# Row-wise largest absolute value of an 8192 x 8192 matrix: SyncE's loads without the waits that VectorE's count implies

## Chip, cores and metric

One core of one Trainium2 chip. The metric is the device time of one execution in microseconds (us), the median over several; the trace's span leaves out some 1.8 us of it.

## The reference

```python
x = np.random.randn(8192, 8192).astype(np.float32)
out = np.linalg.norm(x, ord=np.inf, axis=1)     # per row: the largest |x|
```

## The kernel before

The matrix is read once, 256 MiB, in 8 MB tiles of 128 partitions x 16384 values (two rows for each partition). Three buffers hold them. SyncE issues every load, VectorE reduces each tile, two small stores write the result. The last eight tiles come in smaller and smaller pieces, so that little is left to reduce once the last byte is there.

```python
sbuf = ctx.enter_context(tc.tile_pool(name="sbuf", bufs=BUFS))      # BUFS = 3
...
for a in range(A):                                                  # 24 tiles in all: the bulk
    for n in range(G):
        t = sbuf.tile([P, W + PAD], F32, tag="t")
        nc.sync.dma_start(out=t[:, :W], in_=x_b[a, n])              # L147
        absmax(r_bulk[:, a, n * B : (n + 1) * B], t[:, :W].rearrange(...))
for i, loads in enumerate(TAIL):                                    # 7 tiles in pieces
    t = sbuf.tile([P, W + PAD], F32, tag="t")
    for j, w in enumerate(loads):
        nc.sync.dma_start(out=t[:, at : at + w], in_=x_t[i][:, at : at + w])   # L159
        ...                                                         # reduces into part
...                                                                 # last tile: 13 pieces, L184
nc.sync.dma_start(out=out_t, in_=r_tail[:])                         # L202, the last store
nc.at_finalize(start_first_load_early)
nc.at_finalize(finish_on_pool)
```

The waits are put in by the framework. A load into a used buffer has two kinds: for VectorE's count (the reduce of the old content is done) and for the semaphore of the load that brought that content. In this kernel's trace the loads count up eight DMA semaphores (100 to 107) in turn, and some loads also wait for the load that had their semaphore before. No load or store of SyncE carries more than one wait in that trace; the others sit in 30 EVENT_SEMAPHOREs, one ahead of each of 29 loads and of the last store.

## Time and profile before

| | before |
|---|---|
| time, median of 3 (lowest to highest) | 627.47 us (627.43 to 627.56) |
| span of the profiled run | 625.7 us |
| loads' queue, share of 16 DMA engines | 99.5% |
| VectorE busy | 88% |
| EVENT_SEMAPHOREs ahead of SyncE's loads and last store | 30 |

```profile
L140 DVE TENSOR_REDUCE r_bulk<-t 128x2 f32<-128x16384 f32 x24 | 413.3, 17220 | 69.7 <-DMA t<-in_x_dram 69.7
t<-in_x_dram SPq DMA_DIRECT2D x24, 40.7
q14 instruction: 2, 0.02, 0.0%
```

A reduce takes 17.22 us and VectorE then waits for data, 69.7 us in all. A load of 8 MB takes 40.7 us from issue to landing.

### The profile page before, as it was taken

How to read it: one execution, taken by the hardware profiler on the slowest of the kernel's cores; microseconds unless marked ns; L12 is line 12 of the kernel's file. 1: busy time of each engine (PE TensorE's matmuls, PEld its weight loads, DVE VectorE, ACT ScalarE, POOL GpSimd, SP SyncE). 2: the span in 40 equal slices, each digit the busy share in tenths (PEclk: the TensorE clock that was granted, in tenths of full speed). 3: DMA queues.
4: the chain of work that ended last, by engine and by line, in shares of the span. 5: the costliest groups of instructions: out<-in, count | busy, mean ns of one | idle time of the engine just before them, and what ended most of it. 6: DMA issues, size and time to landing. Idle time of an engine off the chain costs nothing.

```text
span 625.7 us, 205 instructions
## 1 busy us (share of the span) xinstructions
DVE 552.9 (88%) x67; POOL 0.2 (0%) x4
## 2 busy tenths in 40 slices
DVE  0588988889988889888898888988889999999998
POOL 0000000000000000000000000000000000000000
DMA  9999999999999999999999999999999999999997
GB/s 402 469 402 452 419 452 419 448 423 436 436 419 452 411 461 402 469 402 469 402 469 402 461 411 452 419 448 423 444 413 421 444 425 431 436 425 430 424 422 315
DMA packets 9282, 268.49 MB, mean 429 GB/s; under 512 B 1856, under 2 KB 1856, under 8 KB 3392
## 3 DMA queue, kind: packets, MB, share of 16 engines
q1 hardware_dynamic: 8496, 268.45, 99.5%
q10 hardware_dynamic: 784, 0.02, 0.1%
q14 instruction: 2, 0.02, 0.0%
HBM read 268.44 MB, written 0.03 MB: 429 GB/s over the span
## 4 chain that ended last, share of the span: by engine, by line
DMA 67%; DVE 31%; issue 1%; another core or an unknown queue 0%; DVEq 0%; SPq 0%
DMA t<-in_x_dram 67%; DVE r_bulk L140 24%; DVE part L140 6%; DVE t L140 2%; DVEq L230 0%; DVE r_tail L140 0%; SPq L159 0%
## 5 line engine op out<-in xcount | busy, mean ns | idle before, releaser
L140 DVE TENSOR_REDUCE r_bulk<-t 128x2 f32<-128x16384 f32 x24 | 413.3, 17220 | 69.7 <-DMA t<-in_x_dram 69.7
L140 DVE TENSOR_REDUCE part<-t 128x1 f32<-128x8192 f32 (+20 forms) x28 | 121.5, 4410 | 0.3 <-DMA t<-in_x_dram 0.3
L140 DVE TENSOR_REDUCE t<-t 128x1 f32<-128x1664 f32 (+8 forms) x11 | 16.7, 1576 | 0.2 <-DMA t<-in_x_dram 0.2
L140 DVE TENSOR_REDUCE r_tail<-t 128x1 f32<-128x644 f32 (+1 forms) x2 | 1.5, 814 | 0.0
L137 DVE MEMSET part<- 128x56 f32 x1 | 0.1, 105 | 0.9 <-PEq L219 0.9
L140 DVE TENSOR_REDUCE r_tail<-part 128x14 f32<-128x56 f32 x1 | 0.2, 201 | 0.0
L219 POOL MEMSET const-bfloat16-1.0<- 128x1 bf16 x1 | 0.1, 101 | 0.0
L219 POOL MEMSET const-uint8-127<- 128x1 uint8 x1 | 0.1, 101 | 0.0
L219 POOL MEMSET const-float32-0.0<- 128x1 f32 x1 | 0.1, 98 | 0.2 <-issue 0.2
L219 POOL MEMSET const-float32-1.0<- 128x1 f32 x1 | 0.1, 98 | 0.0
## 6 DMA issues: line engine op xcount, KB each, us to landing
t<-in_x_dram SPq DMA_DIRECT2D x2, 3392.0 KB, 37.2
t<-in_x_dram SPq DMA_DIRECT2D x1, 5376.0 KB, 40.5
t<-in_x_dram SPq DMA_DIRECT2D x1, 4864.0 KB, 32.9
t<-in_x_dram SPq DMA_DIRECT2D x1, 4800.0 KB, 32.9
t<-in_x_dram SPq DMA_DIRECT2D x1, 4672.0 KB, 34.7
t<-in_x_dram SPq DMA_DIRECT2D x3, 1536.0 KB, 36.9
t<-in_x_dram SPq DMA_DIRECT2D x1, 3520.0 KB, 42.7
t<-in_x_dram SPq DMA_DIRECT2D x1, 3328.0 KB, 40.4
```

Of the source, the lines that this page charges most:

```text
L137: nc.vector.memset(part[:], 0.0)
L140: return nc.vector.reduce_max(out=o, in_=i, axis=X, apply_absolute_value=True)
L219: nc = _bacc.Bacc("TRN2", target_bir_lowering=False, num_devices=1)
```

## The change

Intent: VectorE's reduce of a tile itself waited for the tile's load. Once VectorE's count says that the reduce is done, the load has landed, and the second wait says nothing new. A pass over the finished program drops it wherever VectorE's waits up to that count cover it.

```diff
+def drop_implied_waits(nc):
+    ...                       # upto[k]: the semaphore values that VectorE had waited for by count k+1
+    for n, i in enumerate(insts):
+        if i.engine != sp or type(i).__name__ != "InstDMACopy":
+            continue
+        waits = i.sync_info.on_wait
+        at = [s.wait_value for s in waits if s.id == counter]
+        if len(waits) > 1 and at:
+            known = upto[max(at) - 1]
+            keep = [s for s in waits
+                    if s.id == counter or s.wait_value > known.get(s.id, 0)]
+            insts[n] = copy.replace(i, sync_info=mybir.SyncInfo(
+                on_wait=keep, on_update=list(i.sync_info.on_update)))
+    body.instructions = insts
 ...
+    nc.at_finalize(drop_implied_waits)
     nc.at_finalize(start_first_load_early)
```

More of the change, by code (lines that the diff above doesn't have):

```diff
@@ L2 @@
+import copy
 import logging
@@ L96, in finish_on_pool @@
     end.instructions = [i for i in insts if i.name not in moved] + [wait, clear]
+def drop_implied_waits(nc):
+    sp, dve = mybir.EngineType.SP, mybir.EngineType.DVE
+    body = nc.main_func.blocks[-2]
+    insts = list(body.instructions)
+    counter, seen, upto = None, {}, []
+    for i in insts:
+        if i.engine != dve or i.sync_info is None:
+            continue
+        for s in i.sync_info.on_wait:
+            assert s.sync_type == "semaphore" and s.wait_mode == "sem-ge-imm"
+            seen[s.id] = max(seen.get(s.id, 0), s.wait_value)
+        for s in i.sync_info.on_update:
+            assert s.update_mode in ("sem-inc", "sem-add-imm")
+            assert counter in (None, s.id)
+            counter = s.id
+            upto += [dict(seen)] * s.update_value
+    for n, i in enumerate(insts):
+        if i.engine != sp or type(i).__name__ != "InstDMACopy":
+            continue
+        waits = i.sync_info.on_wait
+        at = [s.wait_value for s in waits if s.id == counter]
+        if len(waits) > 1 and at:
+            known = upto[max(at) - 1]
+            keep = [
+                s
+                for s in waits
+                if s.id == counter or s.wait_value > known.get(s.id, 0)
+            ]
+            insts[n] = copy.replace(
+                i,
+                sync_info=mybir.SyncInfo(
+                    on_wait=keep, on_update=list(i.sync_info.on_update)
+                ),
+            )
+    body.instructions = insts
 @with_exitstack
```

## The prediction

> **What bounds the kernel now.** I read the page's busy shares and DMA lines first, then stretches of the span, then the chain that ended last, then what SyncE's queue waited for, and at last SyncE's own instructions line by line.
>
> The page:
>
> ```profile
> span 625.7 us, 205 instructions
> DVE 552.9 (88%) x67; POOL 0.2 (0%) x4
> DMA  9999999999999999999999999999999999999997
> q1 hardware_dynamic: 8496, 268.45, 99.5%
> HBM read 268.44 MB, written 0.03 MB: 429 GB/s over the span
> ```
>
> VectorE is busy 88% of the span, the loads' queue q1 99.5% of 16 engines' time. The input is 8192 x 8192 x 4 bytes = 268.4 MB and every byte crosses once, so the time is bytes over rate. The stretches show whether the rate ever falls (columns: stretch, its length and VectorE's busy time, GpSimd's, clock, DMA share, GB/s):
>
> ```profile
> 22.00:60.00 38.00, 34.43 (x2) 0.00 (x0) 1.00 1.00 435
> 200.00:300.00 100.00, 89.43 (x6) 0.00 (x0) 1.00 1.00 433
> 550.00:560.00 10.00, 10.00 (x2) 0.00 (x0) 1.00 0.99 425
> 615.00:620.00 5.00, 5.00 (x5) 0.00 (x0) 1.00 1.02 416
> 620.00:623.00 3.00, 3.00 (x4) 0.00 (x0) 1.00 0.72 261
> ```
>
> The DMA share is about 1.00 in bulk, tail and nearly the last load; it falls only once no load is left. A change can gain only by making the engines move bytes faster, by starting the first load sooner, or by shortening the last 3 us. Does an earlier issue of some load help? The chain, in order of time (start, length, what):
>
> ```profile
> 60.64 17.23 DVE r_bulk L140
> 77.87 0.02 issue
> 77.89 40.76 DMA t<-in_x_dram
> 118.65 0.02 issue
> ```
>
> It looks as if a load's issue were on the path: reduce, 0.02 us, load. But the load takes 40.76 us to land. An 8 MB load (128 x 16384 x 4 = 8.39 MB) at the 434 GB/s of these stretches needs 19.3 us. It therefore lay about 40.8 - 19.3 = 21.4 us behind the load ahead of it. With three buffers one is being reduced, one arrives, one is queued. An issue earlier or later by a fraction of a microsecond changes only the time in the queue, not when the bytes move.
>
> **What the removed waits do today.** SyncE's own waits (total us, times, longest), then its instructions by line (duration in ns min/median/max, first and last start in us):
>
> ```profile
> SPq L147 <- DVE r_bulk L140: 361.6, 21, 17.2
> SPq L147 <- DMA t<-in_x_dram: 54.9, 21, 20.2
> SPq L202 <- DVE r_tail L140: 6.9, 1, 6.9
> ...
> L147 SPq EVENT_SEMAPHORE  x21: 17/17/17, 22.0 to 408.7; - x21
> L159 SPq EVENT_SEMAPHORE  x7: 17/17/28, 428.0 to 544.3; - x7
> L184 SPq EVENT_SEMAPHORE  x1: 17/17/17, 578.0 to 578.0; - x1
> L202 SPq EVENT_SEMAPHORE  x1: 17/17/17, 617.1 to 617.1; - x1
> ```
>
> The instruction that carries the second wait is a separate EVENT_SEMAPHORE ahead of the load. It starts when the load that held the buffer has landed: the first at 22.0 us, where VectorE starts its first reduce (21.99). The fourth load itself starts at 39.2 us, when that reduce is done. So the order is: wait for the landing, run 17 ns, then wait a whole reduce for VectorE. 361.6 / 21 = 17.2 us, which is the reduce's own length (17220 ns). The wait that goes is never the one that ends last.
>
> There are 30 of these instructions in the lines above, and 29 should go. I worked through the wait values of the kernel before with the rule of the diff: all 21 of L147, all 7 of L159 and the one ahead of the last store (L202) are implied by the VectorE count. The one of L184 (578.0 us) stays. It is for a semaphore of a load whose reduce VectorE had not reached by the count that the load waits for, and the load follows at 578.1: there the wait for the DMA really ends last.
>
> [...]
>
> **The change part by part.** Removed: 29 EVENT_SEMAPHOREs of 17 ns (those of L159 up to 28): at most 21 x 17 + 7 x 28 + 17 = 570 ns of SyncE, all beside other work.
> - 21 in the bulk: each ends about 17.2 us before its load may go. On the path: 0. Even were the load issued sooner, 21.4 us of queue lie ahead of it. 0 us.
> - 7 in the tail's loads: VectorE is waited for after them. The profile's waits of that line on VectorE (51.7 us in 3 and 47.7 in 4) give 17.2 and 11.9 us on average. 0 us.
> - 1 ahead of the last store: the EVENT_SEMAPHORE starts at 617.1 us, the store at 624.0, so 6.9 us are spent waiting for the last reduces. This is the one place where an issue lies on the end of the span with no queue ahead of it, and the wait removed ends 6.9 us too early to matter. 0 us.
>
> Added: nothing on the chip; the pass runs while the program is built. Moved: SyncE reaches its wait for VectorE earlier and sits there. The loads, their order, the buffers, the reduces and the first load ahead of the barrier are untouched. Sum: 0.0 us, so 627.47 stays, rounded down to 627.4 because what sign there can be is a gain.
>
> **Rivals.**
> 1. *The separate wait costs at issue although it passed early*[...]. For: one shift of the last store would be seen in full. Against: 17 us lie between the two, and the load follows the reduce's end by 0.02 us in the chain. Were all 29 on the path at the 0.1 us that separate the kept pair at L184 (578.0 to 578.1), the gain would be 2.9 us, 0.46%: 624.6, still within 2%. With the queue taken into account only the store could show it: 0.1 us, 627.4.
> 2. *Some removed wait is really the last one*, so that loads go earlier and the queue fills deeper. Against: a wait implied by VectorE's count cannot end after it, and the waits on VectorE are long (17.2, 11.9 and 6.9 us). Even then the DMA share is already 1.00. [...]
> 3. *Slower*: loads issued in another pattern meet each other or the last store. Against: issue times follow VectorE's counts, which stay. What remains is a different alignment of the 29-instruction-shorter stream, and run-to-run drift. I would give it a few tenths of a microsecond: 627.8.
>
> **Range and chances.** The three runs lie within 0.13 us (627.43 to 627.56), and the profiled one took 627.57. The loading is rate-bound, so the next draw, possibly on another chip, moves with the rate: 0.1% of it is 0.6 us. I take 626.9 to 627.9 for 8 in 10. To leave the 2% band (12.5 us) the DMA would have to lose or gain its rate, which nothing here touches: within 2% at 0.98, 0.01 each for the rest.
>
> **What would show it right or wrong.** Right: the page counts 29 instructions less (176), SyncE's lines show one EVENT_SEMAPHORE at L184's loads and none at the others; the DMA share stays about 1.00 in the same stretches; a bulk load starts still 17.2 us after the landing of the one before it in its buffer, and 0.02 us after the reduce; the span stays within 0.5 us of 625.7. Rival 1 would show as a shorter gap from the last reduce's end to the store; rival 2 as loads that start ahead of where they do now, or q1 over 99.5%; rival 3 as stretches below 430 GB/s in the bulk, or a DMA share below 0.97. I would be wrong if the first load started later or sooner against the barrier, which the diff gives no reason for.

The sum came to 0.0 us: zero for the waits of the bulk, of the tail's loads and of the last store alike, so 627.47 us stayed and was put down as 627.4. Measured: 30 EVENT_SEMAPHOREs, a DMA share of 1.00 while SyncE waits, 433 and 435 GB/s in two stretches of the bulk.

## The result, and the profile after

| | before | after |
|---|---|---|
| time, median of 6 (lowest to highest) | 627.53 us (627.43 to 627.7) | 627.87 us (627.49 to 628.08) |
| ratio, 95% interval | | 1.0004 (0.9992 to 1.0017) |
| span of the profiled run | 625.7 us | 625.9 us |

The ratios and their intervals are not quite the ratios of the medians. The interval holds 1: no difference can be told. The page after:

```profile
span 625.9 us, 176 instructions
q1 hardware_dynamic: 8496, 268.45, 99.5%
q14 instruction: 1, 0.01, 0.0%
```

29 instructions and one packet of the instruction queue less; the other lines stay as they were. The kernel's lines now have other numbers: L187 is the bulk load, L199 the tail's, L224 the last tile's, L242 the store. SyncE's waits (total us, times, longest), and the only EVENT_SEMAPHORE left on those lines (ns min/median/max, start in us):

```profile
SPq L187 <- DVE r_bulk L180: 417.3, 21, 37.5
SPq L242 <- DVE r_tail L180: 9.5, 1, 9.5
...
L224 SPq EVENT_SEMAPHORE  x1: 17/17/17, 578.0 to 578.0; - x1
```

Before, the bulk loads waited 54.9 us for landings and then 361.6 us for VectorE: 416.5 us. Now they wait 417.3 us for VectorE alone. The wait that was dropped became part of the wait that was kept, to a microsecond. For the store it is 2.6 + 6.9 = 9.5 us before, 9.5 after. The chain (start, length, what) and the stretches have not moved either:

```profile
60.63 17.23 DVE r_bulk L180
77.86 0.02 issue
77.88 40.77 DMA t<-in_x_dram
...
22.00:60.00 38.00, 34.43 (x2) 0.00 (x0) 1.00 1.00 435
200.00:300.00 100.00, 89.44 (x6) 0.00 (x0) 1.00 1.00 434
620.00:623.00 3.00, 3.00 (x4) 0.00 (x0) 1.00 0.68 256
```

The same load was issued at 77.89 before and at 77.88 now, and landed after 40.76 and 40.77 us.

Two questions are left. Was the issue of a load really hidden, and by what? And do the medians (0.34 us higher with fewer instructions) mean anything?

### The profile page after: what moved, and what is told of

Same layout as the page of the kernel before. It is cut to its first block, busy times and chain, and to the rows that moved or that the text cites. A ratio compares the mean times of both kernels' runs of the same rounds, so it can differ in the third digit from the quotient of the medians. Undisturbed runs are those within 1.5% of the kernel's fastest.

```text
span 625.9 us, 176 instructions
## 1 busy us (share of the span) xinstructions
DVE 552.9 (88%) x67; POOL 0.2 (0%) x4
## 3 DMA queue, kind: packets, MB, share of 16 engines
q1 hardware_dynamic: 8496, 268.45, 99.5%
## 4 chain that ended last, share of the span: by engine, by line
DMA 67%; DVE 31%; issue 1%; another core or an unknown queue 0%; DVEq 0%; SPq 0%
DMA t<-in_x_dram 67%; DVE r_bulk L180 24%; DVE part L180 6%; DVE t L180 2%; DVEq L271 0%; DVE r_tail L180 0%; SPq L199 0%
```

## The experiments

Eleven kernels ran in three jobs, each job on another chip; all gave the right result. Within a job they share the runs of the kernel before. The padding of most of them is one helper, called after the passes above:

```python
def extra_waits(nc, n, at, on):
    # n EVENT_SEMAPHOREs more on SyncE, ahead of each load (or of the last store) that waits for
    # VectorE. on="vector": they repeat that wait, so they run once VectorE is done.
    # on="landed": they repeat an implied wait, so they run while the load must still wait.
```

### The spread: the changed kernel again, and a copy of the kernel before

Edit: none in either.

> The changed kernel again, unchanged. My theory (the removed waits cost nothing on the path, and the 0.3 us between the two medians is spread): a ratio to the kernel before within 0.9990 to 1.0010, with either sign. The rival that the shorter instruction stream costs a little (few tenths of a us): 1.0003 to 1.0008 once more, clear of an identical copy of the kernel before in the same job.

> A copy of the kernel before as its own control: the same program. The ratio shows what spread alone does: 1.0000 within 0.0010. A difference between this and the changed kernel's ratio of less than 0.0005 can't be told from nothing.

Measured: before 627.54 us (9 runs, 627.4 to 628.2); the changed kernel 627.64, ratio 1.0002 (0.9989 to 1.0014); the copy 627.68, ratio 1.0001 (0.9989 to 1.0014). An identical program stands as far from itself as the changed one does. The 0.34 us of the first comparison is spread; these runs resolve about 0.1%.

### Ten more waits at each load, on either side of VectorE's signal

```diff
 (kernel before)   + nc.at_finalize(lambda nc: extra_waits(nc, 10, "loads", "landed"))
 (kernel after)    + nc.at_finalize(lambda nc: extra_waits(nc, 10, "loads", "vector"))
```

> The kernel before with ten more such EVENT_SEMAPHOREs at each of its 29 loads that have one, for a landing that is already past while the load still has to wait for VectorE: 290 more. My theory: 290 times some 65 ns (the step from the kept one at the tail's first tile to its load) is 19 us of SyncE's time, all inside waits of 9 to 17 us: a ratio within 0.9990 to 1.0010, the loads start 0.02 to 0.03 us after the reduces as before. The rival that a passed wait still costs at issue: ten times what the change removed, up to 19 us, ratio 1.03.

> The changed kernel with ten EVENT_SEMAPHOREs at each of 29 loads that repeat the wait for VectorE, so that they run after the reduce and the load really goes later. My theory: each such load starts some 0.6 us later (10 x 65 ns), still some 20 us ahead of the end of the load in front of it: ratio within 0.9990 to 1.0015, DMA share about 1.00 still. The rival that the chain (reduce, issue, load) is what sets the time: each of the chain's ten or so steps from reduce to load gets 0.6 us longer, 6 us, ratio 1.010; if all 29 count, 19 us, 1.03.

Measured: 628.68 us (ratio 1.0018, 1.0004 to 1.0031) and 628.67 us (1.0017, 1.0005 to 1.003). The timelines, first landed10, then vector10 (start, length, engine, line, operation; the SPq row merges two loads):

```profile
22.15 17.22 DVE L199 TENSOR_REDUCE r_bulk<-t 128x2 f32<-128x16384 f32 x1 [21.16 <-DMA t<-in_x_dram]
39.39 19.62 SPq L206 DMA_DIRECT2D t<-in_x_dram  x2
```

```profile
22.12 17.22 DVE L238 TENSOR_REDUCE r_bulk<-t 128x2 f32<-128x16384 f32 x1 [21.16 <-DMA t<-in_x_dram]
40.00 19.58 SPq L245 DMA_DIRECT2D t<-in_x_dram  x2
```

In the first, the load starts with the reduce's end (22.15 + 17.22 = 39.37). In the second it starts 0.66 us after it (39.34, then 40.00), and so do most of its loads. An EVENT_SEMAPHORE whose wait is met costs 61 ns of SyncE in such a row, though its own record shows 17 to 28 ns: (0.636 - 0.027) / 10 from the trace's starts. Yet both kernels lost the same 1.1 us. Both rivals, which spoke of 6 to 19 us, are refuted; so is my expectation of no loss at all. What the two share is 290 more instructions, and four packets of the instruction queue where the kernels before and after have two and one:

```profile
q14 instruction: 4, 0.03, 0.0%
```

(This is vector10's page.)

### Is it the fetch? The waits on another engine, and four times as many

```diff
 (kernel after)    + nc.at_finalize(lambda nc: waits_on_scalar(nc, 10))    # 290 on ScalarE, by the same counts
 (kernel before)   + nc.at_finalize(lambda nc: extra_waits(nc, 40, "loads", "landed"))
```

> Both ten-fold runs lost 1.1 us (628.7 against 627.5), alike, whether the 290 instructions ran ahead of VectorE's signal or after it; so it can't be the load's issue. New theory: it is their fetch. The trace shows 8192-byte packets of the instruction queue ([...]309 ns each) among the loads: 2 in the kernel before, 1 in the changed one, 4 in each ten-fold run. Here the changed kernel gets 290 EVENT_SEMAPHOREs on ScalarE instead, which issues no load. Fetch theory: 2 or 3 packets more and again 0.6 to 1.5 us more, near 628.7. Rival (SyncE's own stream or its issue is what costs): 627.5 to 627.9 as the changed kernel.

> The kernel before with 40 EVENT_SEMAPHOREs more at each of 29 loads, ahead of VectorE's signal: 1160 more, 40 x 61 ns = 2.4 us of each wait of 9 to 17 us. Fetch theory: some 9 packets more in the instruction queue, at the 0.4 to 0.5 us each that the ten-fold runs had: 3.5 to 5 us more than before, 631 to 632.6, and load starts still 0.03 us after the reduces. Issue theory of the plain kind (each costs its 61 ns): 71 us. A fixed cost for the stream of any length: 628.7 as with ten.

Measured: on ScalarE 628.18 us (627.81 to 628.62), ratio 1.0009 (0.9996 to 1.0021): three packets, a loss of 0.6 us in the median, but the interval holds 1, so these times alone settle nothing. The landings in its trace say more. Set against those of before, they fall back by 0.4 us at the packet at 391.3 us and by 0.7 us more at the one at 507.2: instructions of an engine that issues no load of the matrix cost the same kind of step. With 40 on SyncE: 633.75 us, ratio 1.0098 (1.0084 to 1.0112), 6.2 us more than the 627.58 of before. Its page and chain:

```profile
q1 hardware_dynamic: 8496, 268.45, 98.6%
...
q14 instruction: 11, 0.09, 0.0%
```

```profile
136.67 41.46 DMA t<-in_x_dram
...
254.12 41.44 DMA t<-in_x_dram
295.56 0.02 issue
295.58 17.23 DVE r_bulk L199
312.81 0.02 issue
312.83 40.73 DMA t<-in_x_dram
...
370.83 41.44 DMA t<-in_x_dram
```

Nine packets more for 1160 instructions, so 129 to a packet of 8192 bytes on average, some 64 bytes each. With 42 instructions to a bulk load (itself, its own wait and 40 more), the first five packets come 58.7 us apart, which is about three loads or 126 instructions. The cost is 6.2 / 9 = 0.69 us a packet; I had expected 0.4 to 0.5. The issue is still 0.02 us after the reduce. The chain's loads take 41.45 us where one packet falls into them, or into the load that is under way when they are issued, and 40.73 where none does, the value of before. The trace's packet records say how one packet costs 0.7 us. Columns: start us, end us, length ns, queue, bytes, first of one DMA engine (told from the others by each packet starting where the last ended), then of another in the same time:

```
162.421 164.839 2418 q1  65536
164.835 165.144  309 q14  8192
165.141 167.974 2833 q1  65536
167.971 170.391 2420 q1  65536

164.558 166.976 2418 q1  65536
166.972 169.390 2418 q1  65536
```

The packet of instructions takes 306 ns of that engine, and the load's packet after it 415 ns longer than the others: 0.72 us. Why it takes longer these runs do not show. A load lands when the last of the 16 engines has its share: in before, the first load counts its semaphore up 16 times, from 21.11 to 21.97 us, and its reduce starts at 21.99. The engines do not wait in between: in before, the packet records make 16 rows, which begin at 1.0 to 1.8 us and go on to the last load's end, and in none does a packet start more than 4 ns after the end of the last one. So what one engine loses it keeps to the end. In landed40 it is nearly always the same engine. In the last microseconds of landed40 (columns as in the prediction's stretches) the DMA share is one sixteenth:

```profile
624.00:628.00 4.00, 4.00 (x5) 0.00 (x0) 1.00 0.06 25
```

Fifteen engines are done by 623.1 us, and one still works on its share until 628.7: only an engine that took nearly all of the nine packets can be so far behind. In before all sixteen end between 621.4 and 622.7 us.

### Does a later load cost anything with a load queued ahead? And the one packet that the change saved?

```diff
 (kernel after)    + nc.at_finalize(lambda nc: extra_waits(nc, 40, "loads", "vector"))
 (kernel after)    + nc.at_finalize(lambda nc: extra_waits(nc, 4, "loads", "vector"))
```

> The changed kernel with 40 EVENT_SEMAPHOREs on the wait for VectorE at each of 29 loads: each load goes 2.4 us later, with a load queued ahead of it. My theory: the issue is still hidden (21 us of queue), and only the fetch of 1160 instructions costs: 633 to 634, as the 40 ahead of VectorE's signal did (633.75), steps of 0.7 us in the landings at each packet. If the delay of 2.4 us cost anything of its own: 10 to 71 us more.

> The changed kernel with 4 such EVENT_SEMAPHOREs at each of 29 loads: 116 more, which should be one packet more of the instruction queue, as the kernel before has one more than the changed one. A packet takes one DMA engine 0.3 us and the load packet after it 0.4 us longer: 0.7 us on one engine of 16. Reserve theory: the engine that fetches is not the last of the 16 (their starts lie 0.8 to 1.4 us apart), so the first packet is mostly taken from its reserve: 627.4 to 628.0, no step of 0.7 us in the landings; and that is why the packet that the change saves gained nothing. Linear theory (each packet costs 0.7 us at the end): 628.2 to 628.5.

Measured: vector40 633.38 us, ratio 1.0093 (1.0079 to 1.0107), against landed40's 633.75 in the job before, on another chip (the kernel before took 627.56 us in vector40's job and 627.58 in landed40's). Its bulk loads start 2.45 to 2.91 us after their reduce, where those of landed40 start 0.03 us after it, and it is no slower. Its landings, too, go back in steps of 0.7 us at the packets (the first, at 67.0 us, is free). So the time of issue is worth nothing here, and the whole loss is fetch.

vector4: 627.53 us (627.46 to 627.68) against 627.56, ratio 0.9999 (0.9987 to 1.0012): 116 instructions more and no loss. Its page counts three packets of the instruction queue; by the packet records one of them is a 24-byte one at the start, two have 8192 bytes, at 315.7 and 609.6 us.

```profile
q14 instruction: 3, 0.02, 0.0%
```

No landing moves by more than the usual spread after 315.7. The engine that fetched there had ended its packet first of the 16, the last one 0.8 us later: it had a reserve as large as the 0.72 us that it lost. In scalar10 the engine that fetched at 391.3 us ended 0.40 us ahead of the last one, which leaves 0.32 of 0.72 us, and the landings moved by 0.38. In vector10 the packets at 161, 391 and 578 us moved the landings by about 0.0, 0.6 and 0.7 us: the first one is free, the next are not. The change saves one packet, at 591.9 us. The landings behind it, in us (loads are counted from 0; piece 48 is the first one behind the packet at 609 to 610 us, which both kernels have):

```
piece              41      43      45      47      48
before         594.58  600.31  605.51  609.93  612.33
after          594.57  600.28  605.49  609.91  612.47
```

With or without the saved packet they agree to 0.03 us, so it had cost the kernel before nothing; that its engine had a reserve as in vector4 is inferred. Behind the packet that stays, the kernel after lands 0.14 us later, and this is the difference of the two profiled spans. It is spread: the repeat of after and the copy of before, in the job of the first experiments, landed piece 48 at 612.38 and 612.43. The packet that stays need not be free, either: from piece 47 to 48 before and after take 2.40 and 2.56 us, the copy 1.97.

### What hides the issue: the loads one reduce later

```diff
 (kernel after)    + nc.at_finalize(wait_one_reduce_more)   # 21 bulk loads: VectorE's count + 1
 (the second)      + nc.at_finalize(lambda nc: extra_waits(nc, 40, "loads", "vector"))
```

> The changed kernel, its 21 loads of the bulk made to wait for one reduce of VectorE more, so that each is issued with no other queued, some 2.1 us before the landing of the load that is under way. My theory: what hides the issue is the queued load. With 2.1 us left and some 1.4 us from issue to landing of the small store, the queue just does not run dry or does so by up to 1 us a load: 627.5 to 650, DMA share in the bulk 0.95 to 1.00. The rival that the issue was never covered by the queue but by something else (a reserve in VectorE): no change or a loss of 19 us per load, 1000 us.

> The same with 40 EVENT_SEMAPHOREs on the wait for VectorE at each of 29 loads, so that each load goes 40 x 61 ns = 2.4 us later still, which is more than the 2.1 us left. My theory: now the issue lies on the path and each of the 21 loads costs some 0.5 to 2.5 us over the run before: 10 to 50 us over it, DMA share in the bulk 0.88 to 0.97. If the issue is hidden for another reason: only the fetches, 4 us over the run before.

Measured: 652.48 us (650.37 to 655.05), ratio 1.0398 (1.0375 to 1.0422), and 665.84 us, ratio 1.0614 (1.0597 to 1.063). The middle of the span, in the order before, late, late with 40 waits:

```profile
100.00:400.00 300.00, 268.31 (x16) 0.00 (x0) 1.00 1.00 433
```

```profile
100.00:400.00 300.00, 254.04 (x16) 0.00 (x0) 1.00 0.98 415
```

```profile
100.00:400.00 300.00, 242.25 (x16) 0.00 (x0) 1.00 0.94 396
```

Each load goes 19.3 us later and loses only (652.48 - 627.58) / 21 = 1.2 us in the mean: that much of the delay is not covered by the 2.0 to 5.0 us that remain until the load under way lands. The mean is of unlike loads. By the landings of late's trace, the fourth load, issued 2.1 us ahead of the landing of the one before it, landed 22.3 us behind that one; the fifth, issued 5.0 us ahead, 19.3 us behind, as with a queue. Not all of the loss is idle engines: the rate fell by 4% (433 to 415 GB/s), the share by 2%, and in the loads that lost over 2 us a packet of 65536 bytes took 2.47 to 2.52 us on average in place of 2.42, for a reason that these runs don't show. My expectation gave up to 1 us a load and 650 us at most, so it was a little short. With 2.4 us more, another 13.4 us go. vector40 says what those waits cost by fetch when the issue is hidden: 633.38 - 627.56 = 5.8 us. Some 13.4 - 5.8 = 7.6 us are then the issue itself, 0.4 us a load (a rough figure, as late's own runs lie 4.7 us apart), and the DMA share falls from 0.98 to 0.94. The very padding whose timing was worth nothing behind a queued load costs time without one. It is the third buffer's queued load that hid the issue.

### The last store, where nothing is queued

```diff
 (kernel after)    + nc.at_finalize(lambda nc: extra_waits(nc, 20, "store", "vector"))
```

> The changed kernel with 20 EVENT_SEMAPHOREs on the wait for VectorE ahead of the last store alone, where no load is queued. My theory: here an instruction between VectorE's signal and the issue lies on the path: the store starts 20 x 61 ns = 1.2 us after its 0.03 us, the whole run is 1.2 us longer, 628.8 to 629.0 (no packet of the instruction queue more than one). If even this is hidden: 627.5 to 627.9.

Measured: 629.67 us against 627.56, ratio 1.0034 (1.002 to 1.0047): 2.1 us more, where I had expected 1.2 to 1.4. The end of the timeline after the change, then in this run:

```profile
622.61 1.55 DVE L180 TENSOR_REDUCE r_tail<-t 128x1 f32<-128x644 f32 x2
624.19 0.35 SPq L242 DMA_DIRECT2D out_dram<-r_tail  x1
```

```profile
622.64 1.55 DVE L238 TENSOR_REDUCE r_tail<-t 128x1 f32<-128x644 f32 x2
625.92 0.34 SPq L300 DMA_DIRECT2D out_dram<-r_tail  x1
```

The store starts 1.73 us after the last reduce in place of 0.03. 20 x 61 ns are 1.2 us of it; some 0.5 us are over. Single loads of vector10 and vector4 show a like extra of 0.4 to 0.5 us, each a few us ahead of a packet of instructions; why, these runs do not show. The store then landed 0.2 us later after its issue (1.65 against 1.42), with such a packet beside it. So at this place, alone of those tested with the queue as it is, what stands between VectorE's signal and the issue comes out at the end in full. The wait that the change removed stood ahead of the signal, 6.9 us too early.

## Why the prediction was right

- **No gain in the bulk: right, and shown twice over.** Its step was that the dropped wait ends a reduce ahead of the kept one; the waits before (54.9 + 361.6) became one of 417.3 us. Its second step, that some 21 us of queue ahead of a load hide its issue, is shown by vector40 against landed40 (2.4 us later, no slower) and by the late loads (without the queue a delay costs).
- **The last store as the one exposed issue: right.** The padding of the store appeared at the end, and the dropped wait did not.
- **29 of 30 go, the one at the last tile stays: right,** as counted.
- **Rival 1, a passed wait costs at issue:** refuted; ten and forty of them left the load 0.03 us behind the reduce.
- **Rival 2, deeper queue:** the loads start where they did, and q1 stays at 99.5%.
- **Rival 3, slower by the shorter stream:** I gave it 627.8, and the first median was 627.87. The repeat and the copy (627.64 and 627.68) say that this was spread.
- **What the prediction did not have:** "Added: nothing on the chip" and "all beside other work" left out that instructions came through the same DMA engines that are the bound (q1 at 99.5%): in before, a packet of the instruction queue stands from 591.92 to 592.23 us between two of the loads' on one engine, as in landed40's records. The term is some 0.7 us in landed40 for each packet of about 129 instructions, and here zero, since the one packet saved had moved no landing. It would not have changed the sum, but it is the only way that these runs show in which the 29 instructions touch the bound.
- **The number and the range:** the forecast of 627.4 leaned towards a gain that neither median of the changed kernel (627.87, 627.64) shows. The range, 626.9 to 627.9, holds the 627.87 by 0.03 us, and that is luck: its width came from three runs 0.13 us apart, while nine runs of the kernel before in the next job span 0.8 us (627.4 to 628.2), and three of the six runs of after lie at 627.9 or above.
- **The rate:** the 433 and 435 GB/s of the prediction are two of six stretches of the bulk; the other four read 421 to 439, about the same mean. That no rate is left above this was not shown: no run tests it.

## What to carry to other kernels

Before you remove a wait, look at which of an instruction's waits ends last and what stands ahead of its transfer in the queue: here a wait that ended first was free, and even an issue 2.4 us late was free while another load was queued. Look for such gains where nothing is queued, at the last store (20 waits there cost 2.1 us), or where no load is queued ahead (40 waits a load then cost 13.4 us, against 5.8 us with one queued). In a kernel that is bound by the DMA engines, count instructions in hundreds: here each 129 or so of them were an 8 KB transfer on an engine that the loads need, and once its reserve was gone each such transfer cost 0.7 us.
